# One 512-column matmul for both activation halves in a hybrid decoder trunk, from the first feed-forward on

## The chip, the cores and the metric

One core of a Trainium2 chip runs the whole program. The time is the device time of one execution in microseconds (us), taken as the median of several runs of the same kernel. Lower is better.

## The reference, cut to what matters

Two residual layers over 256 positions of width 2048. Layer 0 mixes with latent attention and gated DeltaNet, layer 1 with gated linear attention (GLA). After each mixer comes a SwiGLU feed-forward of width 5632. Every sub-layer is normalised, then modulated by a shift, a scale and a gate that are linear in SiLU(c).

```python
for layer in range(DEPTH):                      # DEPTH = 2
    shift, scale, gate = ada_modulation(c, ada_w[layer, 0], ada_b[layer, 0])
    h = rms_norm(x, norm_g[layer, 0]) * (1.0 + scale) + shift
    mix = ab_mixer(h, ...) if layer % 2 == 0 else gla_mixer(h, ...)
    x = x + gate * mix
    shift, scale, gate = ada_modulation(c, ada_w[layer, 1], ada_b[layer, 1])
    h = rms_norm(x, norm_g[layer, 1]) * (1.0 + scale) + shift
    x = x + gate * ((silu(h @ w1) * (h @ w3)) @ w2)
return rms_norm(x, final_norm)
```

All of it is float32. D_MODEL is 2048, D_FF is 5632, SEQ is 256.

## The kernel before, in words

**Layout.** Activations are kept transposed: a tile holds 128 features on the partitions and the 256 positions (T = 256) along the free axis. The residual `x` is 16 such tiles.

**Precision.** Every float32 product is made of three matmuls in the float32r format. A weight block w is split into a high part (a cast on ACT, `hi`, L253) and the rest (a subtraction on DVE, `lo`, L193). An activation tile is split likewise and both parts lie side by side in one tile `hl` of shape (128, 2, 256). `mm3` (L261) then issues hi x h0, hi x h1 and lo x h0, each of 256 columns, into the same 256 columns of a PSUM tile. The product lo x h1 is left out.

**Streaming.** `stream_T` (L267) makes 512 output features: it takes four PSUM tiles `acc` of 512 float32 columns each (one bank; the pool has four, so one stream holds them all) and uses the first 256 columns of each. The contraction runs in pieces of four 128-row blocks, called a piece here. For each piece `wload` (L245) starts one DMA of 1 MB (`raw`, three buffers, on SP's queue), casts two halves on ACT and makes two halves of `lo` on DVE (four buffers each for hi and lo, two rows of blocks in one buffer). PE then does, for each of the four output blocks b, four triples `mm3`. So a piece is 48 matmuls. After the last piece of a stream `evac(b, ps)` empties each of the four banks, right after its block. The next stream starts with bank 0.

**The users of `stream_T` from the first feed-forward on.** `ffn` (L1263) runs twice. Its 11 groups of 512 hidden features need one stream over w1 and one over w3, each with 16 blocks of contraction (four pieces). `evac1` applies SiLU from PSUM on ACT; `evac3` multiplies on DVE, then splits the product into h0 (ACT, L223) and h1 (DVE). `ffn2` (L1295) runs w2 in four column groups for 12, 12, 12 and 8 blocks of contraction, and empties with `x_add` (one `scalar_tensor_tensor` on DVE, L200, which adds gate times PSUM to `x`). In layer 1, `gla_in` (L1305) has two streams for q, two for k and four for r (evacuations at L1343, L1345 and L1358); its values come from `gla_v` (L1361), which does not use `stream_T`: there the activation block is the stationary operand, and the weight parts of 512 columns move. `out_proj` (L1243) has four streams with 16 blocks. That makes 2 x (11 x 2 x 64 + 44 x 16) = 4224 triples in the two feed-forwards and 4 x 64 + 4 x 64 + 4 x 64 = 768 in layer 1's mixer, 4992 in all.

**What sets the order.** The rows of `ada_w` (201 MB) are streamed in the background: `tick` is called in every `wload` and steps a generator that issues a DMA of 1 MB (`araw`) on SP's queue and multiplies its rows on DVE (`ada`, L200, two instructions of 1024 columns a step) or on PE. In the first feed-forward its rate is RF0 = 1.5 a piece. Each engine executes in order; the order on each engine is fixed when the kernel is built, by the framework's own estimate of the timeline (`schedule_with_timeline_sim=True`), except that the `ada` steps keep the program's order where `s.keep` is set. At the beginning of each sub-layer `h_tile` makes the 16 `hl` tiles (DVE, ACT for h0, DVE for h1). At the end of layer 0's feed-forward and of both mixers `x_square` squares each new `x` tile on ACT and sums on POOL (`ss`, L193) and PE. The GLA heads (`gla_scores`, `gla_pv`) are woven between the streams of `gla_in`.

Of the kernel before, what the change touches and what calls it, by code (L numbers as in the profile page):

```python
# [13 lines left out]
AF = mybir.ActivationFunctionType  # L14
ALU = mybir.AluOpType
# [4 lines left out]
T = 256  # L20
# [109 lines left out]
class Trunk:  # L130
    def __init__(s, ctx, tc, h, dbg=None, stop=None):
        s.tc, s.nc, s.h, s.dbg, s.stop = tc, tc.nc, h, dbg or {}, stop
        s.cp = ctx.enter_context(tc.tile_pool(name="cp", bufs=1))
        s.rawp = ctx.enter_context(tc.tile_pool(name="rawp", bufs=3))
        s.hlp = ctx.enter_context(tc.tile_pool(name="hlp", bufs=NHL))
        s.arp = ctx.enter_context(tc.tile_pool(name="arp", bufs=NAR))
        s.dp = ctx.enter_context(tc.tile_pool(name="dp", bufs=NDP))
        s.tp = ctx.enter_context(tc.tile_pool(name="tp", bufs=4))
        s.accp = ctx.enter_context(tc.tile_pool(name="accp", bufs=4, space=PSUM))
        s.smp = ctx.enter_context(tc.tile_pool(name="smp", bufs=3, space=PSUM))  # L140
        s.pap = ctx.enter_context(tc.tile_pool(name="pap", bufs=1, space=PSUM))
        s.drp = ctx.enter_context(tc.tile_pool(name="drp", bufs=1, space=bass.MemoryType.DRAM))
        s.n = 0
        s.bg = s.pin = None
        s.mr = None
        s.xg, s.sq = [], []
        s.keep = KP[0]
        s.done = set()
        s.gq = False
        s.fin, s.ends = [], []  # L150
        s.cap = 1 << 30
        s.rate = s.due = 0.0
# [108 lines left out]
    def mm3(s, ps, w, hl, start, stop):  # L261
# [2 lines left out]
        s.mm(ps, w[0], hl[:, 1], False, False)  # L264
        s.mm(ps, w[1], hl[:, 0], False, stop)

    def stream_T(s, src, k0, hs, c0, ncol, evac, nk=None, prepare=None):  # L267

        nb = ncol // 128
        nk = nk or len(hs)  # L270
        ps = [s.acc() for _ in range(nb)]
        for t in range(0, nk, 4):
            n = min(4, nk - t)
            ws = s.wload(src, k0 + t, n, c0, ncol, TI)
            if not TI:
                s.tick(s.rate)
            if prepare is not None:
                prepare(t)
            for b in range(nb):
                for q in range(n):  # L280
                    w = tuple(x[:, b * 128:(b + 1) * 128] for x in ws[q])
                    s.mm3(ps[b][:, :T], w, hs[t + q], t + q == 0, t + q == nk - 1)
                if t + n == nk:
                    evac(b, ps[b][:, :T])
                yield

    def stream_few(s, src, k0, hs, c0, ncol, evac):
# [193 lines left out]


    def x_add(s, l, m, k, ps):
        s.stt(s.x[:, k], ps, s.gate(l, m, k), s.x[:, k], ALU.mult, ALU.add)

    def x_square(s, k):

# [775 lines left out]
    def ffn(s, l):  # L1263
        r = s.x_rstd()
        hs = [s.h_tile(l, 1, k, r) for k in range(KT)]
        s.tick(NF)
        w1, w3, w2 = s.h["ffn_w1"][l], s.h["ffn_w3"][l], s.h["ffn_w2"][l]
        chunks = [(0, 3), (3, 6), (6, 9), (9, 11)]
        pend = None
        for ci, (g0, g1) in enumerate(chunks):  # L1270
            gt = []
            for g in range(g0, g1):
                sl = [None, None]

                def evac1(b, ps):
                    if b % 2 == 0:
                        sl[b // 2] = s.d((128, 2, T))
                    s.act(sl[b // 2][:, b % 2], ps, AF.Silu)
                yield from s.stream_T(w1, 0, hs, 512 * g, 512, evac1)

                def evac3(b, ps):
                    t = sl[b // 2][:, b % 2]
                    s.tt(t, ps, t, ALU.mult)
                    hl = s.d((128, 2, T), F32R)
                    s.split(hl, t)
                    gt.append(hl)
                yield from s.stream_T(w3, 0, hs, 512 * g, 512, evac3)
                if pend is not None:
                    yield from s.ffn2(l, w2, *pend)
                    pend = None  # L1290
            pend = (4 * g0, gt, ci == len(chunks) - 1)
        s.lnexp()
        yield from s.ffn2(l, w2, *pend)
# [11 lines left out]
    def gla_in(s):  # L1305
        nc = s.nc
        w = s.h["gla_w_in"][0]
        r = s.x_rstd()
        s.hs = hs = [s.h_tile(1, 0, k, r) for k in range(KT)]
        s.tick(NF)  # L1310
        def gates():
            ps = s.acc()
            for c in range(4):
                s.stream_narrow([(w, 6144, 16)], 4 * c, hs[4 * c:4 * c + 4], ps, c == 0, c == 3)
            g17 = s.tmp((32, T))
            nc.vector.memset(g17, 1.0)
            nc.vector.tensor_copy(g17[:16], ps[:16, :T])
            wg = [s.d((17, 512)) for _ in range(2)]
            for hf in range(2):
                nc.sync.dma_start(wg[hf][0:16], s.h["gla_w_gk2"][0][:, hf * 512:(hf + 1) * 512])  # L1320
                nc.sync.dma_start(wg[hf][16:17], s.h["gla_b_gk2"][:, hf * 512:(hf + 1) * 512])
            s.ls = {}
            for hf in range(2):
                for t in range(2):
                    p = s.sm()
                    s.mm(p, g17[:17, t * 128:(t + 1) * 128], wg[hf])
                    a = s.d()
                    s.act(a, p, AF.Abs)
                    s.act(a, a, AF.Exp, scale=-1.0)
                    s.act(a, a, AF.Ln, bias=1.0)  # L1330
                    s.stt(a, p, 0.0, a, ALU.min, ALU.subtract)
                    s.ts(a, a, 1.0 / 16.0, ALU.mult)
                    s.ls[hf, t] = a

        s.gq, s.gk, s.gv = {}, {}, {}
        for g in range(2):
            for nme, c0, dst in (("q", 0, s.gq), ("k", 1024, s.gk)):
                def evac(b, ps):
                    key = 2 * g + b // 2
                    if b % 2 == 0:  # L1340
                        dst[key] = s.d((128, 2, T))
                    if nme == "q":
                        s.act(dst[key][:, b % 2], ps, AF.Copy, scale=1.0 / 16.0)  # L1343
                    else:
                        nc.vector.tensor_copy(dst[key][:, b % 2], ps)  # L1345
                yield from s.stream_T(w, 0, hs, c0 + 512 * g, 512, evac)
                if g == 0 and nme == "q":
                    gates()
            yield ("qk", g)
        for g in range(4):  # L1350
            yield from s.gla_v(w, g)
        s.gr = {}
        for g in range(4):
            def evac(b, ps):
                key = 2 * g + b // 2
                if b % 2 == 0:
                    s.gr[key] = s.d((128, 2, T))
                (nc.scalar.copy if b % 2 else nc.vector.tensor_copy)(s.gr[key][:, b % 2], ps)  # L1358
            yield from s.stream_T(w, 0, hs, 4096 + 512 * g, 512, evac)

    def gla_v(s, w, g):  # L1361
# [165 lines left out]
    def run(s):  # L1527
# [43 lines left out]
        if s.stop == "x0":  # L1571
            return
        s.rate = RF0
        s.keep = KP[2]
        s.gq = GQ
        s.cap = 1 << 30
# [66 lines left out]
```

## Time and profile before

| | |
|---|---|
| median of 3 runs | 2623.29 us (2622.99 to 2635.62) |
| the profiled execution's own time | 2625.56 us |
| its span, first to last instruction | 2623.8 us |
| mean granted TensorE clock | 0.988 |
| PE / weight load / DVE / ACT / POOL busy | 98% / 93% / 65% / 44% / 4% |
| moved by DMA | 622.67 MB, mean 237 GB/s |

A busy engine is one with an instruction in flight. Matmuls overlap in the profile: an instruction's duration is longer than the distance from its start to the next one's, so the pace of a stretch is its length divided by its count, not the mean duration. The chain of waits is followed back from the last instruction, so its pieces are the work that set the end.

### The profile page before, as it was taken

What the parts mean: (1) busy time and instruction counts of PE and PEld (TensorE: products, weight loads), DVE (VectorE), ACT (ScalarE), POOL (GpSimd) and SP (SyncE); (2) the same over time, 40 slices, a digit from 0 to 9 for tenths busy, and PEclk for the clock granted to TensorE, in tenths of its full rate; (3) what the DMA queues carried; (4) which work ended last, traced back from release to release, by engine and by line L of the source; (5) the groups of instructions that cost most, each with busy time, mean ns of one, the idle gap of its engine ahead of it and who ended that gap; (6) DMA issues with size and microseconds to landing.
All of it is one profiled execution on the core that took longest, in us unless ns stands there. A gap on an engine that the chain in (4) does not pass through costs nothing.

```text
span 2623.8 us, 48907 instructions
## 1 busy us (share of the span) xinstructions
PE 2571.5 (98%) x20794; PEld 2439.8 (93%) x20794; DVE 1698.8 (65%) x2271; ACT 1157.2 (44%) x1699; POOL 98.9 (4%) x154
## 2 busy tenths in 40 slices
PE   8999998999999999999999999999999999999998
PEld 5799886799999999999998988999999999999998
DVE  3667754688878787777787777865644544544444
ACT  4435664545443343334345434663534334334334
POOL 0000014001000000000011000001000000000001
PEclk9999998999999999999999999999999999999999
DMA  9975666776889888888885555445555555555553
GB/s 348 358 284 165 219 244 254 273 289 222 325 292 344 314 309 317 316 301 316 319 303 209 193 177 192 162 160 177 160 178 187 182 180 190 178 183 188 178 190 115
DMA packets 262280, 622.67 MB, mean 237 GB/s; under 512 B 17119, under 2 KB 28012, under 8 KB 241582
## 3 DMA queue, kind: packets, MB, share of 16 engines
q1 hardware_dynamic: 259902, 608.32, 66.6%
q0 software_dynamic: 1968, 11.14, 1.2%
q8 instruction: 163, 2.67, 0.4%
q14 instruction: 55, 0.45, 0.0%
q10 hardware_dynamic: 192, 0.08, 0.0%
HBM read 616.09 MB, written 3.41 MB: 236 GB/s over the span
## 4 chain that ended last, share of the span: by engine, by line
PE 96%; DVE 2%; ACT 1%; issue 1%; DMA 0%; POOL 0%; SPq 0%; DVEq 0%; ACTq 0%; POOLq 0%
PE acc L190 87%; PE sm L190 6%; PE pa L190 3%; DVE lo L193 1%; ACT hi L253 0%; DVE ada L200 0%; DMA d<-in_x 0%; DMA araw<-in_ada_w 0%; ACT tmp L203 0%; POOL ss L193 0%; PE sm L556 0%; DVE tmp L193 0%; ACT d L203 0%; DVE d L193 0%; POOL d L193 0%
## 5 line engine op out<-in xcount | busy, mean ns | idle before, releaser
L190 PE MATMUL acc<-d,hi 128*128 128x256 f32 x12000 | 2182.6, 285 | 11.0 <-ACT d L203 9.6
L190 PEld LDWEIGHTS acc<-d,hi 128*128 128x128 f32 x12000 | 1871.8, 193 | 46.6 <-ACT d L203 12.8
L190 PE MATMUL acc<-d,lo 128*128 128x256 f32 x6000 | 1685.0, 285 | 3.2 <-DVE lo L193 3.2
L193 DVE TENSOR_TENSOR lo<-raw,hi 128x1024 fp32r<-128x1024 f32 (+2 forms) x801 | 941.6, 1204 | 641.0 <-ACT hi L253 622.1
L253 ACT CAST hi<-raw 128x1024 fp32r<-128x1024 f32 x776 | 782.5, 1046 | 1055.2 <-PE acc L190 912.5
L190 PEld LDWEIGHTS acc<-d,lo 128*128 128x128 f32 x6000 | 1146.4, 193 | 11.9 <-DVE lo L193 4.7
L200 DVE SCALAR_TENSOR_TENSOR ada<-araw,sc,ada 128x1024 f32<-128x1024 f32 x240 | 299.9, 1287 | 6.2 <-DMA araw<-in_ada_w 6.0
L200 DVE SCALAR_TENSOR_TENSOR x<-acc,mod,x 128x256 f32<-128x256 f32 x192 | 87.5, 480 | 66.4 <-PE acc L190 66.4
L193 DVE TENSOR_TENSOR d<-acc,d 128x256 f32<-128x256 f32 (+1 forms) x168 | 79.8, 485 | 64.9 <-PE acc L190 63.1
L190 PE MATMUL acc<-hi,d 128*128 128x512 f32 (+1 forms) x320 | 95.2, 375 | 0.0
L190 PE MATMUL pa<-araw,sc 128*32 128x512 f32 x480 | 73.9, 617 | 3.6 <-DMA araw<-in_ada_w 2.2
L190 PEld LDWEIGHTS acc<-hi,d 128*128 128x128 f32 x320 | 57.8, 189 | 10.7 <-ACT d L1172 0.8
L223 ACT CAST d<-d 128x256 fp32r<-128x256 f32 x128 | 47.8, 404 | 43.6 <-DVE d L193 43.5
L193 DVE TENSOR_TENSOR d<-d,d 128x256 fp32r<-128x256 f32 (+1 forms) x155 | 60.8, 421 | 8.5 <-ACT d L203 4.1
L203 ACT ACTIVATE d<-acc 128x256 f32<-128x256 f32 x96 | 36.7, 382 | 56.6 <-PE acc L190 56.4
L190 PE MATMUL acc<-lo,d 128*128 128x512 f32 (+1 forms) x160 | 59.0, 369 | 0.0
L193 POOL TENSOR_TENSOR ss<-ss,tmp 128x256 f32<-128x256 f32 x44 | 50.5, 1148 | 73.4 <-ACT tmp L203 71.5
L193 DVE TENSOR_TENSOR tmp<-d,tmp 128x512 f32<-128x512 f32 x64 | 43.9, 686 | 6.1 <-issue 3.3
L492 POOL COPY ss<-tmp 128x256 f32<-128x256 f32 x3 | 2.6, 880 | 997.6 <-ACT tmp L203 997.6
L203 ACT ACT_TABLE_LOAD x29 | 37.2, 1283 | 2.2 <-PEq L1632 0.7
L203 ACT ACTIVATE d<-tmp,mod 128x256 fp32r<-128x256 f32 x64 | 29.3, 502 | 20.2 <-DVE tmp L200 15.4
L190 PEld LDWEIGHTS sm<-d,d 32*32 32x32 f32 (+2 forms) x368 | 30.5, 152 | 8.3 <-issue 2.9
(214 smaller groups left out, 1022.9 us busy)
## 6 DMA issues: line engine op xcount, KB each, us to landing
raw<-in_ffn_w SPq DMA_DIRECT2D x264, 1024.0 KB, 5.2
araw<-in_ada_w SPq DMA_DIRECT2D x175, 1024.0 KB, 7.3
raw<-in_gla_w_in SPq DMA_DIRECT2D x48, 1024.0 KB, 5.1
raw<-in_ab_w_in SPq DMA_DIRECT2D x30, 1024.0 KB, 5.3
raw<-in_ab_w_out SPq DMA_DIRECT2D x16, 1024.0 KB, 5.1
raw<-in_gla_w_out SPq DMA_DIRECT2D x16, 1024.0 KB, 5.0
raw<-in_ab_w_in SPq DMA_DIRECT2D x20, 512.0 KB, 7.8
araw<-in_ada_w POOLq DMA_DIRECT2D x9, 1024.0 KB, 5.2
```

The costliest lines, as they stand in the source:

```text
L190: s.nc.tensor.matmul(out, lhsT=lhsT, rhs=rhs, start=start, stop=stop)
L193: (eng or s.nc.vector).tensor_tensor(out=out, in0=a, in1=b, op=op)
L200: return s.nc.vector.scalar_tensor_tensor(out=out, in0=a, scalar=sc, in1=b, op0=op0, op1=op1)
L203: s.nc.scalar.activation(out, a, f, **kw)
L223: s.nc.scalar.copy(hl[:, 0], x)
L253: s.nc.scalar.copy(hi[:, :n, :ncol], raw[:, a:a + n, :ncol])
L492: s.nc.gpsimd.tensor_copy(s.ss, q)
```

## The change

Until the first feed-forward the kernel is as before. From there a flag `s.two` is set. `stream_T` then calls `mmw` for each triple: one matmul of 512 columns, in which the high weight part meets h0 and h1 side by side and fills all 512 columns of the bank, and one of 256 columns, lo x h0, which adds into the first half. For the first contraction block the wide one comes first, for all others the narrow one does. The two halves of the bank are added on emptying: `join` copies the second half on ACT and adds the first on DVE; `x_add` does its instruction once for each half. The evacuations of w1, w3, q, k and r use `join`, with SiLU, the product or the scale applied behind it in SBUF. `gla_v` and everything of layer 0's mixer stay as they are.

```diff
+    def mmw(s, ps, w, hl, first, last):
+        both = hl.rearrange("p a t -> p (a t)")
+        if first:
+            s.mm(ps, w[0], both, True, False)
+            s.mm(ps[:, :T], w[1], hl[:, 0], False, False)
+        else:
+            s.mm(ps[:, :T], w[1], hl[:, 0], False, False)
+            s.mm(ps, w[0], both, False, last)
+
+    def join(s, out, ps):
+        s.nc.scalar.copy(out, ps[:, T:])
+        s.tt(out, ps[:, :T], out, ALU.add)
...
-                    s.mm3(ps[b][:, :T], w, hs[t + q], t + q == 0, t + q == nk - 1)
+                    if two:
+                        s.mmw(ps[b], w, hs[t + q], t + q == 0, t + q == nk - 1)
+                    else:
+                        s.mm3(ps[b][:, :T], w, hs[t + q], t + q == 0, t + q == nk - 1)
                 if t + n == nk:
-                    evac(b, ps[b][:, :T])
+                    evac(b, ps[b] if two else ps[b][:, :T])
...
     def x_add(s, l, m, k, ps):
-        s.stt(s.x[:, k], ps, s.gate(l, m, k), s.x[:, k], ALU.mult, ALU.add)
+        for a in range(0, ps.shape[-1], T):
+            s.stt(s.x[:, k], ps[:, a:a + T], s.gate(l, m, k), s.x[:, k], ALU.mult, ALU.add)
...
-                    s.act(sl[b // 2][:, b % 2], ps, AF.Silu)
+                    a = sl[b // 2][:, b % 2]
+                    if s.two:
+                        s.join(a, ps)
+                        ps = a
+                    s.act(a, ps, AF.Silu)
...
                     t = sl[b // 2][:, b % 2]
+                    if s.two:
+                        u = s.tmp((128, T))
+                        s.join(u, ps)
+                        ps = u
                     s.tt(t, ps, t, ALU.mult)
...
+                    o = dst[key][:, b % 2]
+                    s.join(o, ps)
                     if nme == "q":
-                        s.act(dst[key][:, b % 2], ps, AF.Copy, scale=1.0 / 16.0)
-                    else:
-                        nc.vector.tensor_copy(dst[key][:, b % 2], ps)
+                        s.act(o, o, AF.Copy, scale=1.0 / 16.0)
...
-                (nc.scalar.copy if b % 2 else nc.vector.tensor_copy)(s.gr[key][:, b % 2], ps)
+                s.join(s.gr[key][:, b % 2], ps)
...
         s.rate = RF0
+        s.two = True
```

## Rows read from the trace of the kernel before

**Rows 1.** The page's busy times: us, share of the span, instructions.
```profile
PE 2571.5 (98%) x20794; PEld 2439.8 (93%) x20794; DVE 1698.8 (65%) x2271; ACT 1157.2 (44%) x1699; POOL 98.9 (4%) x154
```

**Rows 2.** The page's chain that ended last, by engine and by line.
```profile
PE 96%; DVE 2%; ACT 1%; issue 1%; DMA 0%; POOL 0%; SPq 0%; DVEq 0%; ACTq 0%; POOLq 0%
```

**Rows 3.** Stages: length, busy us by engine (instructions), PE clock, DMA share, GB/s.
```profile
core 0: us, PE busy (x) PEld busy (x) DVE busy (x) ACT busy (x) POOL busy (x), PEclk, DMA share, GB/s
618.90:1397.00 778.10, 776.02 (x6432) 769.15 (x6432) 610.13 (x646) 311.64 (x390) 16.57 (x12) 1.00 0.85 312
1402.00:1480.00 78.00, 77.42 (x601) 74.61 (x602) 54.66 (x83) 38.73 (x59) 2.27 (x6) 0.96 0.50 170
1480.00:1660.00 180.00, 176.28 (x1094) 159.79 (x1093) 136.01 (x206) 78.16 (x108) 3.55 (x7) 0.98 0.54 183
1660.00:1745.00 85.00, 85.00 (x692) 84.14 (x691) 64.46 (x102) 59.88 (x80) 0.00 (x0) 1.00 0.49 158
1745.00:1845.50 100.50, 96.85 (x798) 95.20 (x797) 58.63 (x79) 48.68 (x74) 13.40 (x12) 1.00 0.55 181
1845.50:2609.00 763.50, 763.45 (x6339) 763.34 (x6339) 377.90 (x442) 310.83 (x395) 10.79 (x12) 1.00 0.55 176
```

**Rows 4.** PE's idle time from 590 us on, by releaser: us, times, longest.
```profile
PE acc L190 <- ACT d L203: 9.4, 3, 3.7
PE sm L190 <- DVE tmp L193: 3.5, 1, 3.5
PE acc L1511 <- ACT d L203: 1.8, 1, 1.8
PE sm L190 <- POOL ss L193: 1.6, 1, 1.6
PE sm L190 <- ACT tmp L436: 1.5, 1, 1.5
PE sm L190 <- ACT tmp L203: 1.4, 2, 1.2
PE acc L190 <- DVE x L200: 0.5, 1, 0.5
```

**Rows 5.** Chain pieces in the feed-forwards (256 columns): start us, us, what.
```profile
918.54 92.25 PE acc L190 x768
...
1845.55 763.40 PE acc L190 x6336
```

**Rows 6.** Chain pieces inside `gla_v` (512 columns, weights moving).
```profile
1583.71 15.45 PE acc L190 x68
...
1600.05 6.36 PE acc L190 x28
```

**Rows 7.** Groups by shape, 1480 to 1660 us: us busy, mean ns | idle before.
```profile
L190 PE MATMUL acc<-hi,d 128*128 128x512 f32 x256 | 82.2, 396 | 0.0
L190 PE MATMUL acc<-lo,d 128*128 128x512 f32 x128 | 50.0, 390 | 0.0
```

**Rows 8.** Groups by shape over the last feed-forward, 1845.5 to 2609 us.
```profile
L200 DVE SCALAR_TENSOR_TENSOR x<-acc,mod,x 128x256 f32<-128x256 f32 x64 | 29.5, 480 | 35.0 <-PE acc L190 35.0
L193 DVE TENSOR_TENSOR d<-acc,d 128x256 f32<-128x256 f32 x44 | 18.0, 423 | 12.4 <-PE acc L190 11.2
L203 ACT ACTIVATE d<-acc 128x256 f32<-128x256 f32 x44 | 16.8, 382 | 25.0 <-PE acc L190 25.0
```

**Rows 9.** DVE's timeline late in layer 0's feed-forward.
```profile
1306.11 2.36 DVE L193 TENSOR_TENSOR lo<-raw,hi 128x1024 fp32r<-128x1024 f32 x2 [0.85 <-ACT hi L253]
1308.39 2.48 DVE L200 SCALAR_TENSOR_TENSOR ada<-araw,sc,ada 128x1024 f32<-128x1024 f32 x2
1311.87 2.36 DVE L193 TENSOR_TENSOR lo<-raw,hi 128x1024 fp32r<-128x1024 f32 x2 [1.00 <-ACT hi L253]
...
1354.52 2.48 DVE L200 SCALAR_TENSOR_TENSOR ada<-araw,sc,ada 128x1024 f32<-128x1024 f32 x2
1356.91 1.66 DVE L200 SCALAR_TENSOR_TENSOR x<-acc,mod,x 128x256 f32<-128x256 f32 x4
1358.48 2.35 DVE L193 TENSOR_TENSOR lo<-raw,hi 128x1024 fp32r<-128x1024 f32 x2
```

**Rows 10.** One stretch of layer 0's feed-forward in which DMA is full (columns as rows 3).
```profile
1310.00:1320.00 10.00, 10.00 (x86) 10.00 (x85) 7.98 (x7) 4.38 (x5) 0.00 (x0) 1.00 1.02 360
```

**Rows 11.** The chain at the end of layer 0's feed-forward.
```profile
1381.22 0.75 DVE x L200 x2
...
1385.73 1.60 POOL ss L193
...
1387.41 1.61 POOL ss L193
...
1389.10 1.59 POOL ss L193
```

**Rows 12.** DVE making h1 in `h_tile`, from 590 us on.
```profile
L200 DVE SCALAR_TENSOR_TENSOR d<-tmp,mod,d 128x256 fp32r<-128x256 f32 x48 | 21.8, 480 | 0.2 <-ACT d L203 0.2
```

**Rows 13.** ACT's timeline in a w1 stream's last piece, layer 0.
```profile
1155.64 0.38 ACT L203 ACTIVATE d<-acc 128x256 f32<-128x256 f32 x1 [1.37 <-PE acc L190]
1156.36 0.38 ACT L203 ACTIVATE d<-acc 128x256 f32<-128x256 f32 x1 [0.34 <-PE acc L190]
1157.56 0.38 ACT L203 ACTIVATE d<-acc 128x256 f32<-128x256 f32 x1 [0.82 <-PE acc L190]
1158.04 2.00 ACT L253 CAST hi<-raw 128x1024 fp32r<-128x1024 f32 x2
1159.94 0.38 ACT L203 ACTIVATE d<-acc 128x256 f32<-128x256 f32 x1
```

More of the change, by code (lines that the diff above doesn't have):

```diff
@@ L148, in __init__ @@
         s.done = set()
-        s.gq = False
+        s.gq = s.two = False
         s.fin, s.ends = [], []
@@ L270, in stream_T @@
         nk = nk or len(hs)
+        two = s.two
         ps = [s.acc() for _ in range(nb)]
```

## The prediction, made before the changed kernel ran

> **What bounds the kernel now.** I read the busy times first. PE has an instruction in flight for 98% of the span, the weight loads for 93%, DVE for 65%, ACT for 44% [rows 1]. Matmuls overlap, so this alone is no proof; the chain of waits is: 96% of the span is PE's own work [rows 2]. By stages, PE is full in both feed-forwards and in most of layer 1's mixer [rows 3], and from 590 us on it idles for some 20 us in all, the longest single wait being 3.7 us [rows 4]. So a shorter sequence on PE shortens the run, as long as what feeds and empties it keeps up. The margins differ by stage: in layer 0's feed-forward DVE is busy for 610 of 778 us (78%) and DMA at 0.85, in the last one DVE for 378 of 764 us (49%) and DMA at 0.55 [rows 3].
>
> **What a matmul costs.** The pace is length over count. With 256 columns it is 92.25 us / 768 = 120.1 ns in layer 0's feed-forward and 763.40 us / 6336 = 120.5 ns over the whole last one, its slow start included [rows 5]. With 512 columns it is 15.45 us / 68 = 227.2 ns, and 6.36 us / 28 = 227.1 ns [rows 6, 7]. Thus 256 more columns cost 107.1 ns, which is 2.4 GHz, and the remainder, 120.1 - 107.1 = 13.0 ns, is paid once for each matmul with its weight load, however wide it is. The columns of a triple stay the same (3 x 256 = 512 + 256); one matmul and one weight load go. The triple before takes 3 x 120.1 = 360.3 ns, after 120.1 + 227.2 = 347.3 ns.
>
> The Trainium skill ("TensorE: Matmul & The Clock Gate", section "Back-to-back issue gap") gives an isolated warm gap of N/2.4 + 2.5 ns, so a fixed part of only 2.5 ns. By it the term below would be 4992 x 2.5 = 12.5 us. The trace disagrees: 120.1 ns at 256 columns, not 109, and the sum goes by the trace.
>
> **The sum, part by part.**
> Triples: 2112 in each feed-forward and 768 in layer 1's mixer, 4992 in all (the 6336 matmuls of the last one are 3 x 2112 [rows 5]). 4992 x 13.0 ns = **-64.9 us**: 27.5 in each feed-forward, 10.0 in the mixer.
>
> Emptying on ACT: one more copy for each block of w1, w3, q, k and some of r, 0.38 us each [rows 8]. In a feed-forward that is 88 x 0.38 = 33 us on an engine that is busy for 312 of 778 us [rows 3]. Its idle time covers that: 0. If the cover were gone, the next stream's first block would wait for its bank (third rival).
>
> Emptying on DVE: in a feed-forward 88 adds of 0.42 us and 64 second `x_add` of 0.48 us [rows 8], 68 us. In the last feed-forward that makes 446 of 735 us, covered. In layer 0's it makes 678 of some 755 us, 90%. Locally it is tighter: one full piece there runs from 1306.11 to 1311.87 us, 5.76 us, of which DVE idles 1.00 [rows 9], so 4.76 us of work. A w2 stream of three such pieces needs 14.3 us, with four `x_add` of 0.41 us (four in 1.66 us [rows 9]) 15.9 of 17.3 us; after the change 14.3 + 3.3 = 17.6 of 16.7 us. It is short by 0.9 us, if `ada` runs in every piece at this density; the mean of 78% says that it doesn't. The split weights are made ahead of PE, so some lateness costs nothing. Bounds: 0, and 0.9 us for each of 16 w2 streams, 14 us. Before, PE waited for an `x_add` there just once, for 0.5 us [rows 4]. Nearer the low end: **+4 us**. What is late then is lo, which `mmw` uses first, and behind it SP's queue: a raw buffer is free only when its lo is done.
>
> DMA: in layer 0's feed-forward 312 GB/s [rows 3] become 312 x 778 / 755 = 322 GB/s. 360 GB/s have been moved in a stretch in which the engines were full and PE never stopped [rows 10]. 0, and the cover is three raw buffers; without it the first rival.
>
> End of layer 0's feed-forward: here the chain leaves PE and runs over `x_add`, the squares and the sum on POOL [rows 11]. A group of four `x_add` grows by 1.6 us, the last block by 0.4, and lo and `ada` stand in the same queue. Bounds: 0 and 16 x 0.41 = 6.6, with the last block 7 to 8 us. I take **+3 us**, about the part that lies on the chain.
>
> Other ends: one `x_add` more behind the last block of the mixer and of the last feed-forward: 2 x 0.41 = **+0.8 us**.
>
> Starts of the three sub-layers: the first matmul now needs h1 too, which DVE makes behind ACT's h0: 0.48 us [rows 12], three times, **+1.4 us**.
>
> Layer 1's mixer: DVE gets 8 adds for q and 8 for r (k's and half of r's replace a copy) and 16 second `x_add`, 14 us on an engine that is at 76% in the woven part (136 of 180 us [rows 3]). Bounds 0 and 6 us; PE waited once for the heads' DVE work there, 3.5 us [rows 4]. **+2 us**.
>
> Order in PE's queue: the first triple of a stream is wide, narrow, all others narrow, wide. No instruction is added and lo came in time before (no wait of PE for lo is left [rows 4]): 0.
>
> Sum: -64.9 + 4 + 3 + 0.8 + 1.4 + 2 = **-53.7 us**. The profiled execution took 2625.6 us (span 2623.8 and 1.8 around it) and would take 2571.9; it lies 2.3 us above the median of 2623.3, so I forecast **2570 us**, -2.0%.
>
> **The rivals.**
> First: layer 0's feed-forward doesn't follow. DVE at 90%, or the transfers behind it, become the bound there, and the 27.5 us of that stage come back. For it: the 0.9 us by which a full w2 stream is short, and the DMA share of 0.85. Against: the stage's mean. -64.9 + 27.5 + 8 (its end) + 0.8 + 1.4 + 4 = -23: 2600 us. Chance 0.11.
>
> Second: PE gains nothing. No row alternates 512 and 256 columns, and none moves an activation tile of 512 columns; if such a matmul costs as much as two narrow ones (or is carried out as two), the triple stays at 360.3 ns and the additions remain: 2623.3 + 11.2 = 2634.5 us, +0.4%. Against: in `gla_v` wide matmuls are single instructions at 227 ns [rows 6, 7]. Chance 0.08.
> By the 2.5 ns of the Trainium skill's page named above it would be 2623.3 - 12.5 + 11.2 = 2622 us, within 0.5% too; [rows 5, 6] speak against it, and its chance is part of this 0.08.
>
> Third, slower: the banks come free too late. `join` needs ACT, then DVE, before a bank is free. ACT executes in order, and at the end of a stream it also has the pair of casts, 2.0 us, which starts only when PE releases the buffers in the stream's last block. Now three SiLUs go ahead of that pair and one behind it [rows 13]. If the order is fixed so that bank 0's copy stands behind the pair, then with the figures of that stretch it starts at 1160.04 and the add ends at 1160.04 + 0.38 + 0.42 = 1160.84 us, while block 3 ends at about 1157.56 + 1.44 = 1159.0 us and PE wants bank 0. That is 1.9 us, and up to 2.4 more if DVE has begun an `ada` pair [rows 9]; at 3.1 us for each of the 52 streams with `join` it is 161 us: 2731 us. It decides from 53.7 / 52 = 1.0 us a stream on; over 1.3 us it is slower by more than 0.5%. Against: in today's order the emptying instructions go as soon as their block is done. Chance 0.06.
>
> **How the numbers follow.** My forecast has 0.75. The range goes down to 2556 us (all of the 64.9 us, the starts paid, and some 4 us of the waits at the end of layer 0's feed-forward, which are retimed, gone too) and up to 2600 us, which is the upper bounds together (-64.9 + 14 + 8 + 0.8 + 1.4 + 6 = -34.7: 2589 us) and the first rival. A change within 0.5% (13 us) is about what can't be told from none. Faster: 0.75 + 0.11 = 0.86; same 0.08; slower 0.06.
>
> **What would show it.** Right: chain pieces in the last feed-forward of some 174 ns for each matmul (347 / 2) and a length of that stage of 734 to 737 us; 12,000 - 2 x 4992 narrow hi matmuls left and 4992 wide ones; DVE near 90% in layer 0's feed-forward, which takes about 755 us up to its end; PE's idle time not above some 30 us. First rival: waits of PE for lo, or of ACT for raw, in that stage, and its length near 775. Second: a triple still at 360 ns. Third: PE waiting for DVE's adds at the beginning of streams, in the last feed-forward too. I am wrong if the last feed-forward, which has room everywhere, does not get shorter by about 27 us.

## The result, and the profile after the change

The changed kernel takes 2686.4 us (median of 4 runs, 2679.2 to 2688.4), the kernel before 2626.0 us (4 runs, 2623.0 to 2635.6): ratio 1.0223, 95% interval 1.0206 to 1.0239. It is **slower** by 2.2%; forecast was 2570 us. The profiled execution spans 2685.6 us.

Three instructions that make `rs` stand at the starts of the three sub-layers, so the stages can be read from VectorE's timeline of the kernel after:

```profile
621.36 0.42 DVE L200 SCALAR_TENSOR_TENSOR rs<-tmp,tmp 128x256 f32<-128x256 f32 x1
...
1474.29 0.42 DVE L200 SCALAR_TENSOR_TENSOR rs<-tmp,tmp 128x256 f32<-128x256 f32 x1
...
1922.41 0.43 DVE L200 SCALAR_TENSOR_TENSOR rs<-tmp,tmp 128x256 f32<-128x256 f32 x1
```

In the profile before they start at 616.39, 1400.97 and 1843.91 us. From one to the next, and from the last to the span's end:

| stage, us | before | after | change | forecast |
|---|---|---|---|---|
| up to the layer-0 feed-forward | 616.4 | 621.4 | +5.0 | 0 |
| layer-0 feed-forward | 784.6 | 852.9 | **+68.3** | -20.0 |
| layer-1 mixer | 442.9 | 448.1 | +5.2 | -7.1 |
| last feed-forward and end | 779.9 | 763.2 | **-16.7** | -26.6 |

The sum is the difference of the spans, 61.8 us. The 5.0 us lie ahead of the change; in the other profiles below the first stage starts anywhere from 617.1 to 621.6 us, so they are scatter. The loss that counts is in the layer-0 feed-forward; the mixer's +5.2, where a gain was forecast, is taken up in e11 and e13. The page after, busy times and the chain by engine:

```profile
PE 2559.8 (95%) x15802; PEld 2185.3 (81%) x15802; DVE 1821.6 (68%) x2607; ACT 1226.7 (46%) x1897; POOL 91.3 (3%) x154
...
PE 86%; DVE 8%; ACT 2%; issue 2%; DMA 1%; POOL 0%; SPq 0%; DVEq 0%; ACTq 0%; POOLq 0%
```

VectorE has 8% of the chain, 2% before [rows 2]. The windows of the three stages (columns as in [rows 3]):

```profile
624.40:1476.60 852.20, 785.40 (x4322) 669.64 (x4322) 667.43 (x808) 345.95 (x483) 10.76 (x13) 0.96 0.78 284
1476.60:1925.10 448.50, 431.14 (x2410) 373.20 (x2410) 326.49 (x499) 231.38 (x342) 17.38 (x24) 0.98 0.52 174
1925.10:2669.60 744.50, 741.95 (x4230) 644.50 (x4230) 432.98 (x588) 340.10 (x477) 11.30 (x12) 1.00 0.53 180
```

PE idles 852.2 - 785.4 = 66.8 us in the first one (2.1 us in the nearest window before [rows 3]), and its mean granted clock is 0.96 instead of 1.00. VectorE is busy for 667 of 852 us, 78%, as before: not full. DMA's share fell from 0.85 to 0.78: transfers are not what is late. The waits name VectorE's `x_add` (us in all, times, longest):

```profile
PE acc L190 <- DVE x L200: 45.5, 14, 7.8
PE acc L190 <- DVE d L193: 7.8, 3, 3.2
...
PE acc L190 <- DVE lo L193: 1.1, 1, 1.1
```

Fourteen times, where the stage has 16 w2 streams; before it was once, 0.5 us [rows 4]. One of them, on VectorE's timeline of the kernel after (a w2 stream ends, PE's last block is done at about 833.3 us):

```profile
824.62 2.36 DVE L193 TENSOR_TENSOR lo<-raw,hi 128x1024 fp32r<-128x1024 f32 x2 [1.09 <-ACT hi L253]
826.90 2.47 DVE L200 SCALAR_TENSOR_TENSOR ada<-araw,sc,ada 128x1024 f32<-128x1024 f32 x2
829.29 2.35 DVE L193 TENSOR_TENSOR lo<-raw,hi 128x1024 fp32r<-128x1024 f32 x2
831.56 2.47 DVE L200 SCALAR_TENSOR_TENSOR ada<-araw,sc,ada 128x1024 f32<-128x1024 f32 x2
833.96 0.47 DVE L200 SCALAR_TENSOR_TENSOR x<-acc,mod,x 128x256 f32<-128x256 f32 x1
834.35 1.21 DVE L193 TENSOR_TENSOR lo<-raw,hi 128x1024 fp32r<-128x1024 f32 x1
835.48 1.26 DVE L200 SCALAR_TENSOR_TENSOR x<-acc,mod,x 128x256 f32<-128x256 f32 x3
836.66 1.21 DVE L193 TENSOR_TENSOR lo<-raw,hi 128x1024 fp32r<-128x1024 f32 x1
837.79 1.65 DVE L200 SCALAR_TENSOR_TENSOR x<-acc,mod,x 128x256 f32<-128x256 f32 x4
```

Here the planner (the framework's own estimate of the timeline, which fixes the order on each engine) put the first halves of all four banks first (one, then three), then the four second halves. So bank 0, the one that PE wants next, is free only after the **fifth** `x_add`, at about 838.2 us, with two lo between. In nine of the 14 waits PE goes on right behind the fifth `x_add` of the stream. Before, each `x_add` frees its bank, bank 0's with the first, whether the four stand in one run [rows 9], as in 11 of the 16 streams, or with lo and `ada` between. PE's timeline there:

```profile
838.41 0.76 PE L190 MATMUL acc<-d,hi 128*128 128x512 f32 x1 [5.06 <-DVE x L200]
...
840.04 0.63 PE L190 MATMUL acc<-d,hi 128*128 128x512 f32 x1
...
840.68 0.63 PE L190 MATMUL acc<-d,hi 128*128 128x512 f32 x1
...
848.66 0.28 PE L190 MATMUL acc<-d,lo 128*128 128x256 f32 x1
...
849.01 0.28 PE L190 MATMUL acc<-d,lo 128*128 128x256 f32 x1
...
863.17 0.76 PE L190 MATMUL acc<-d,hi 128*128 128x512 f32 x1 [5.51 <-DVE x L200]
```

After standing still for 5.06 us, PE makes a triple in 0.64 us (840.04 to 840.68), by 848.66 in 0.35 us. The windows show the granted clock beside it (the third number from the right):

```profile
836.00:841.00 5.00, 2.59 (x8) 2.33 (x9) 3.44 (x7) 0.00 (x0) 0.00 (x0) 0.52 0.92 345
841.00:846.00 5.00, 5.00 (x25) 4.25 (x25) 0.00 (x0) 0.00 (x0) 0.00 (x0) 0.80 0.32 121
846.00:858.00 12.00, 11.65 (x67) 9.85 (x65) 9.82 (x10) 5.36 (x6) 0.00 (x0) 1.00 0.43 151
```

1.00 is the level of 2.4 GHz; 0.52 is almost all at the level of 1.2 GHz (768 columns in 0.64 us). So a late bank can cost twice: a stream of 48 triples takes 863.17 - 838.41 = 24.8 us, of which PE stands still for 5.5 us and loses some 2 us by running at the lower level (24.8 - 5.5 - 48 x 0.3535 = 2.3). The trace has the clock at that level in 12 stretches of this stage, with PE busy in them for 46.6 us (before: 3.4 us). Eight of the 12 begin in one of the 14 waits or at most 1.5 us behind it; after the other six the clock stayed up.

The pace of the new triple (chain pieces: start, us, what; the fourth is a w2 stream of the last feed-forward):

```profile
949.33 62.35 PE acc L190 x352
...
1185.97 92.56 PE acc L190 x524
...
1925.18 196.70 PE acc L190 x1120
...
2121.99 16.99 PE acc L190 x96
...
2173.37 150.66 PE acc L190 x864
```

In the last feed-forward 150.66 / 432 = 348.8 ns (forecast 347.3, before 361.4 by 763.40 / 2112 [rows 5]). In the layer-0 feed-forward, in stretches without a wait, 62.35 / 176 = 354.3 and 92.56 / 262 = 353.3 ns, so only 7 ns are gained there.

### The profile page after: what moved, and what is told of

Its sections match the earlier page's. It is cut to its first block, busy times and chain, and to the rows that moved or that the text cites. A ratio compares the mean times of both kernels' runs of the same rounds, so it can differ in the third digit from the quotient of the medians.

```text
span 2685.6 us, 39255 instructions
## 1 busy us (share of the span) xinstructions
PE 2559.8 (95%) x15802; PEld 2185.3 (81%) x15802; DVE 1821.6 (68%) x2607; ACT 1226.7 (46%) x1897; POOL 91.3 (3%) x154
## 4 chain that ended last, share of the span: by engine, by line
PE 86%; DVE 8%; ACT 2%; issue 2%; DMA 1%; POOL 0%; SPq 0%; DVEq 0%; ACTq 0%; POOLq 0%
PE acc L190 79%; PE sm L190 5%; DVE lo L193 3%; DVE ada L200 2%; PE pa L190 2%; ACT hi L253 1%; DVE x L200 1%; DMA araw<-in_ada_w 0%; DVE tmp L193 0%; DVE d L200 0%; DVE tmp L200 0%; DVE d L193 0%; ACT tmp L203 0%; DMA d<-in_x 0%; DMA d<-in_ada_w 0%
## 5 line engine op out<-in xcount | busy, mean ns | idle before, releaser
L190 PE MATMUL acc<-d,hi 128*128 128x512 f32 (+2 forms) x7008 | 2137.9, 369 | 71.4 <-DVE x L200 46.2
L190 PE MATMUL acc<-d,lo 128*128 128x256 f32 x6000 | 1635.6, 284 | 4.3 <-DVE lo L193 4.3
L190 PEld LDWEIGHTS acc<-d,hi 128*128 128x128 f32 (+1 forms) x7008 | 1244.1, 191 | 309.6 <-issue 73.3
L200 DVE SCALAR_TENSOR_TENSOR x<-acc,mod,x 128x256 f32<-128x256 f32 x336 | 147.4, 477 | 38.7 <-PE acc L190 37.6
L193 DVE TENSOR_TENSOR d<-acc,d 128x256 f32<-128x256 f32 (+1 forms) x200 | 92.7, 474 | 71.5 <-PE acc L190 40.3
L203 ACT ACTIVATE d<-d 128x256 f32<-128x256 f32 (+1 forms) x138 | 63.0, 467 | 46.6 <-DVE d L193 26.0
L280 ACT COPY d<-acc 128x256 f32<-128x256 f32 x120 | 43.8, 370 | 45.1 <-PE acc L190 43.1
L280 ACT COPY tmp<-acc 128x256 f32<-128x256 f32 x88 | 32.5, 370 | 33.5 <-PE acc L190 33.4
L203 ACT ACTIVATE tmp<-x 128x256 f32<-128x256 f32 x64 | 26.0, 413 | 42.7 <-DVE x L200 42.1
L203 ACT ACTIVATE tmp<-tmp 128x512 f32<-128x512 f32 (+2 forms) x47 | 26.9, 573 | 33.6 <-DVE tmp L193 25.7
```

What stands on the lines that cost most here:

```text
L190: s.nc.tensor.matmul(out, lhsT=lhsT, rhs=rhs, start=start, stop=stop)
L193: (eng or s.nc.vector).tensor_tensor(out=out, in0=a, in1=b, op=op)
L200: return s.nc.vector.scalar_tensor_tensor(out=out, in0=a, scalar=sc, in1=b, op0=op0, op1=op1)
L203: s.nc.scalar.activation(out, a, f, **kw)
L280: s.nc.scalar.copy(out, ps[:, T:])
```

## The experiments

Two theories stood at the outset. A: the banks of the w2 streams come free late, because of where their readers stand in VectorE's list. B: VectorE, which also does the `ada` work, has too much to do in the layer-0 feed-forward.

All times in us; stages as in the table above, from one profiled execution each, so that their sum is not the median; each ratio is against runs of the kernel before on the same chip, with its 95% interval.

| run | layer-0 ff | mixer | last ff | median | ratio |
|---|---|---|---|---|---|
| before | 784.6 | 442.9 | 779.9 | 2626.0 | 1 |
| after | 852.9 | 448.1 | 763.2 | 2686.4 | 1.0223 [1.0206, 1.0239] |
| e1 last ff only | 785.7 | 444.9 | 762.6 | 2613.3 | 0.9952 [0.9934, 0.9971] |
| e2 pairs by bank | 858.1 | 454.4 | 761.6 | 2694.3 | 1.0259 [1.0240, 1.0279] |
| e3 w2 narrow | 793.9 | 453.1 | 766.2 | 2630.4 | 1.0009 [0.9994, 1.0024] |
| e4 x_add from a copy | 798.8 | 454.9 | 767.3 | 2640.3 | 1.0058 [1.0039, 1.0076] |
| e5 first streams narrow | 850.8 | 448.1 | 763.7 | 2682.2 | 1.0206 [1.0191, 1.0221] |
| e6 all banks by ScalarE | 789.8 | 455.2 | 773.2 | 2638.8 | 1.0040 [1.0026, 1.0055] |
| e7 ada rate 1.0 | 789.5 | 462.1 | 782.5 | 2652.6 | 1.0094 [1.0077, 1.0111] |
| e8 = e5 + e6 + e7 | 780.0 | 476.2 | 781.1 | 2659.8 | 1.0120 [1.0105, 1.0136] |
| e9 best mix | 781.4 | 443.7 | 766.9 | 2610.0 | **0.9923 [0.9902, 0.9944]** |
| e10 one reader | 802.8 | 452.2 | 759.2 | 2635.9 | 1.0029 [1.0015, 1.0044] |
| e11 mixer only | 787.7 | 451.6 | 779.6 | 2636.9 | 1.0032 [1.0020, 1.0045] |
| e12 no second x_add | 785.8 | 453.6 | 763.5 | 2619.6 | 0.9959 [0.9944, 0.9974] |
| e13 out_proj only | 784.7 | 441.7 | 779.0 | 2625.6 | 0.9996 [0.9982, 1.0010] |
| e14 e1, last w2 narrow | 785.6 | 448.0 | 761.7 | 2610.7 | 0.9951 [0.9933, 0.9969] |

How far a stage's length scatters is seen where its code is that of before: the layer-0 feed-forward 784.6 to 787.7 (five profiles), the mixer 442.9 to 448.0 (four), the last feed-forward 779.0 to 779.9 (three).

**e1: wide in the last feed-forward alone.**
```diff
-        s.two = True          # after s.rate = RF0
+        s.two = True          # before drain(s.ffn(1))
```
(q, k and r are emptied as before where `s.two` is false.)

> The wide matmul is used in layer 1's feed-forward alone, where DVE has room. Both theories: that stage takes about 744 us as in the changed kernel, against 763.5 before, and nothing else moves: about 2626 - 19 = 2607 us. If the wide matmul were no cheaper on PE, the time would stay at 2626 or rise.

2613.3 us, with a last stage of 762.6, as in the changed kernel: the gain there is independent of the rest, and smaller than the 27.5 us that were forecast. This alone is faster than both kernels.

**e2: x_add in pairs, bank by bank.**
```diff
+            ins = s.stt(...)
+            if s.two and a == 0 and k % 4:
+                s.tc.keep_in_program_order(ins)
```

> Changed kernel, with the same instructions; only DVE's order is bound so that a bank's two x_add stand before the next bank's first one (in the changed kernel all four first halves come first, so that bank 0 is freed after five x_add and the lo instructions between them). Theory A (order: bank 0 is freed late): layer 0's feed-forward gets 15 to 40 us shorter, 2646 to 2671 us in all; not all of it, since lo instructions still stand between bank 0's two. Theory B (load: DVE has too much work in that stage in any order): within 10 us of the changed kernel, 2676 to 2696.

2694.3 us: no gain, which by what was expected is theory B's range. The order did change as meant: in ten of the 11 waits for `x_add` that are left in the stage, PE goes on right behind the stream's second one, no longer the fifth. But lo and `ada` still stand between the two `x_add` of bank 0 (at the place shown above two lo, and the wait there falls only from 5.06 to 3.89 us), and the waits add up to 39.3 us instead of 45.5. So the bank comes nearly as late as in the changed kernel, and this run alone can't tell A from B. e10 puts the question again.

**e3: three matmuls in all w2 streams of both feed-forwards.**
```diff
+            s.two = False
             yield from s.stream_T(w2, k0, gt, 512 * cg, 512, evac)
+            s.two = True
```

> Changed kernel, but the w2 streams use three narrow matmuls and one x_add again. The PE gain of 2 x 704 = 1408 triples is given up (1408 x 12 ns = 17 us). Theory A: the waits for the second x_add go, w1, w3 and GLA keep their gain: 2590 to 2605 us. Theory B: the joins alone (37 us more DVE work in layer 0's feed-forward) still hold PE up: 2615 to 2650.

2630.4 us: 56 of the 60 us come back. But the layer-0 feed-forward, with wide w1 and w3, is still 9 us longer than before.

**e4: x_add from a whole copy that ScalarE makes of the bank.**
```diff
+        u = s.tmp()
+        s.nc.scalar.copy(u, ps)
-            s.stt(s.x[:, k], ps[:, a:a + T], ...)
+            s.stt(s.x[:, k], u[:, a:a + T], ...)
```

> Changed kernel, but for x_add ACT copies the whole bank of 512 columns to SBUF and DVE's two x_add read from there, so that ACT alone frees the bank; DVE has as much work as in the changed kernel. Theory A: PE no longer waits for x_add: 2570 to 2600 us. Theory B: DVE is as loaded as before, PE then waits for lo: over 2650.

2640.3 us, between the two. VectorE has as many `x_add` as in the changed kernel, but reads no bank there, and the stage gets 54 us shorter. So its load alone is not the cause; that the bank waits for it is. From about 1354 us on, the end of the stage, the chain leaves PE and runs largely over lo and `ada`, ScalarE's copies, the `x_add` and ScalarE's squares.

**e5: the first stream of each stage narrow.**
```diff
+                s.two = g > 0
                 yield from s.stream_T(w1, 0, hs, 512 * g, 512, evac1)
+                s.two = True          # and so for the first q stream
```

> Only the first weight stream of each of the three stages (the first w1 stream of both feed-forwards, the first q stream of the mixer) goes back to three matmuls of 256 columns. Theory S (a 512-column first matmul needs the second activation part at once, and VectorE makes those one by one while TensorE waits and loses its clock): each stage start gets 3 to 6 us shorter, 2666 to 2677 us, and the waits of TensorE for the activation tiles at 622, 1476 and 1925 us fall from 2 to 5 us each to under 2. Rival (the start is set by VectorE's list of activation tiles, whichever part is used first): no change, 2680 to 2690 us.

2682.2 us, the rival's range. From `rs` to the first matmul the three starts take 2.5, 1.6 and 1.6 us again, 0.5 to 1.1 us less than in the changed kernel; in the lengths of the stages this can't be told from scatter.

**e6: every wide bank copied whole by ScalarE, joins included.**
```diff
     def join(s, out, ps):
-        s.nc.scalar.copy(out, ps[:, T:])
-        s.tt(out, ps[:, :T], out, ALU.add)
+        u = s.tmp()
+        s.nc.scalar.copy(u, ps)
+        s.tt(out, u[:, :T], u[:, T:], ALU.add)
```

> Each wide bank is copied whole by ScalarE to a tile (x_add and the other emptyings), VectorE then works from that tile alone; the number of VectorE instructions is unchanged. Theory A (what costs the time is that banks are freed by VectorE, whose queue is in order and late): better than the kernel in which only x_add was changed so, 2640 us: 2610 to 2632 us, and TensorE's waits for VectorE's join in the layer-0 feed-forward and the mixer are gone. Rival B (VectorE has too much work in these stages, wherever the bank is freed): 2636 to 2646 us, with TensorE's waits now on the weights' low parts.

2638.8 us, rival B's range. Against e4, the joins' part gains 9 us in the layer-0 feed-forward (798.8 to 789.8), where PE no longer waits for a join, but for lo 5.2 us instead of 4.1; and the last feed-forward loses 6 (767.3 to 773.2), 10 against the changed kernel. Why that one gets longer stays open.

**e7: ada work spread otherwise.** `RF0, RG = 1.0, 1.0` instead of `1.5, 0.5`.

> The changed kernel with the interleaved ada work spread otherwise: 1.0 instead of 1.5 steps per weight load in the layer-0 feed-forward and 1.0 instead of 0.5 in the mixer. Theory B (VectorE's load in the layer-0 feed-forward is what makes the banks late): some 60 of 186 ada steps of 1.2 us leave that stage, its w2 streams recover, 2640 to 2670 us. Theory A (only the order in which a bank's two additions stand in VectorE's list counts): 2680 to 2692 us.

2652.6 us, theory B's range. 124 instead of 186 `ada` instructions of 1.28 us stand in the layer-0 feed-forward, and it falls by 63 us. The mixer takes 60 instead of 24 of them and gets 14 us longer; the last stage takes 26 instead of none and gets 19 longer.

**e8: e5, e6 and e7 together.**

> The three edits of the other kernels of this set together: ScalarE frees every wide bank, the first streams are narrow, the ada work is spread evenly. If bank release, stage starts and VectorE's load are the three causes and add up: 2580 to 2605 us, faster than the kernel before, with the layer-0 feed-forward at 755 to 770 us and the mixer at 435 to 443. If one of them is not a cause, or a fourth is there: above 2612 us.

2659.8 us, a clear miss: the layer-0 feed-forward comes to 780.0, but the mixer to 476.2. PE waits there 12.7 us for ScalarE's products of the heads, 7.3 at a time. The edits don't add up; that each takes from an engine that the next one needs is the likely reason, not a measured one.

**e9: best mix.**
```diff
+        if s.l0:                      # layer-0 feed-forward: as e6
+            ...
+        else:
+            s.nc.vector.tensor_reduce(out=out, in_=ps.rearrange("p (a t) -> p t a", a=2), ...)
+                s.two = l == 1 or g > 0        # w1
+            s.two = l == 1                     # w2
```
(`x_add` as in e10, `s.two` off in the mixer.)

> Meant as the best mix: wide in the last feed-forward (a bank is emptied by one VectorE reduction that adds the halves, so that no ScalarE copy is added) and in w1 and w3 of the layer-0 feed-forward except its first stream (banks freed by a whole ScalarE copy); w2 of the layer-0 feed-forward and the whole mixer stay at three matmuls. If the layer-0 feed-forward can keep the gain of its w1 and w3 streams once VectorE frees no bank late: that stage 766 to 774 us instead of 784.6, the mixer 443 to 446, the last one 757 to 762 instead of 779.9, together 2588 to 2602 us. If the joins alone fill VectorE in that stage: 785 to 795 us for it and 2608 to 2622 us.

2610.0 us, 0.9923 of the kernel before and faster than both kernels, but short of what was expected in both feed-forwards. In the first one PE idles for 6.7 us in all, as little as before (6.9), and still only 3 us are gained. Two rows account for them: the slower pace of the wide triple there, 1344 x 7.0 ns = 9.4 us instead of 17.5, and `ada`'s own matmuls, which take 13.2 us instead of 6.4 (last section).

**e10: two VectorE instructions as before, but only one reads the bank.**
```diff
+        u = s.tmp((128, T))
+        s.nc.vector.tensor_reduce(out=u, in_=ps.rearrange("p (a t) -> p t a", a=2), ...)
+        s.stt(s.x[:, k], u, s.gate(l, m, k), s.x[:, k], ALU.mult, ALU.add)
```

> The changed kernel; x_add adds the two halves with one VectorE reduction into a tile and then adds the gated tile to x: two VectorE instructions for each bank as in the changed kernel, but only the first one reads the bank, so a bank is free after one instruction, as in the kernel before. Theory A (the second reader of the bank, far down VectorE's list, is what frees it late): the layer-0 feed-forward falls from 852.9 to 785 to 800 us, 2615 to 2640 us in all. Theory B (VectorE's load, however the bank is read): 835 to 860 us for that stage, 2670 to 2695 us.

2635.9 us. This decides between A and B. VectorE's timeline at the place shown above, in this kernel:

```profile
830.09 2.47 DVE L200 SCALAR_TENSOR_TENSOR ada<-araw,sc,ada 128x1024 f32<-128x1024 f32 x2
832.48 0.68 DVE L509 TENSOR_REDUCE tmp<-acc 128x256 f32<-128x512 f32 x1
833.08 1.21 DVE L193 TENSOR_TENSOR lo<-raw,hi 128x1024 fp32r<-128x1024 f32 x1
834.21 1.88 DVE L509 TENSOR_REDUCE tmp<-acc 128x256 f32<-128x512 f32 x3
836.01 1.21 DVE L193 TENSOR_TENSOR lo<-raw,hi 128x1024 fp32r<-128x1024 f32 x1
837.14 1.67 DVE L200 SCALAR_TENSOR_TENSOR x<-tmp,mod,x 128x256 f32<-128x256 f32 x4
```

The reductions stand where the four first `x_add` stood, the `x_add` where the four second ones did (this timeline runs 1.5 us ahead of the other); bank 0 is free at 833.1 us instead of 838.2. And the waits of PE in that stage:

```profile
PE acc L190 <- DVE tmp L509: 10.6, 10, 1.8
```

10.6 us instead of 45.5, though VectorE does more work (684.8 us busy instead of 667.4, since a reduction takes 683 ns and the `x_add` behind it 538, where each of the two `x_add` took 476). So 852.9 - 802.8 = 50 us are the price of the second reader; the stage came 3 us above the range that theory A gave. That e7 gains as much is no evidence for load as such: with fewer `ada` instructions the list ahead of the second readers is shorter, so they too come earlier (PE's waits for `x_add` there: 18.2 us).

**e11: wide in the mixer alone**, `s.two` set before the mixer and cleared after it.

> Wide matmuls in the layer-1 mixer alone (q, k, r and the output projection), both feed-forwards as before. The prediction's terms for the mixer were 10 us gained and 2 us for its emptying: 2612 to 2620 us. If the joins put ScalarE and VectorE behind in the woven heads, as the changed kernel's mixer of 448.1 us against 442.9 says: 2627 to 2636 us.

2636.9 us, 10 more (5 to 12 by the interval) instead of 8 less; the mixer takes 451.6. The waits of PE in it, beside those of before in [rows 4], where 3.5 us is all for the heads on VectorE and 1.4 on ScalarE:

```profile
PE sm L190 <- DVE tmp L193: 6.0, 2, 4.2
PE sm L190 <- ACT tmp L203: 5.4, 3, 4.7
```

**e12: no second x_add in the layer-0 feed-forward** (so the product of the high weight part with the low activation part isn't added there).
```diff
+        n = T if (l, m) == (0, 1) else ps.shape[-1]
+        for a in range(0, n, T):
```

> The changed kernel without the second x_add in the layer-0 feed-forward: there the high weight part times the low activation part isn't added in the w2 streams, so x is a little off; the matmuls are all still issued. VectorE has one instruction for each bank again. If the second x_add (as a reader of the bank and as load together) is the whole loss of the w2 streams: the layer-0 feed-forward at 775 to 790 us instead of 852.9, 2610 to 2625 us. If the 512-column matmuls or the joins of w1 and w3 are at fault as well: over 800 us, 2635 us or more.

2619.6 us, as expected: 67 us of the stage hang on these 64 instructions, 50 of them, by e10, on where they release the bank; the other 17 were not divided further. The joins and 512-column matmuls alone leave the stage where it was (785.8).

**e13: wide in the output projection alone.** `s.two` set just before `out_proj` of the mixer.

> Wide matmuls in the mixer's output projection alone (256 of the mixer's 768 triples); q, k, r and both feed-forwards as before. Theory W (the mixer loses in its woven part, where q, k and r are joined beside the heads): the output projection keeps its gain of about 3 us less some tenths at its streams' ends, the mixer takes 439 to 442 us against 442.9 to 444.9, 2622 to 2627 us in all. Rival (the loss sits in the output projection, whose x_add reads each bank twice): the mixer takes 447 to 452 us, 2631 to 2637 us.

2625.6 us with a mixer of 441.7: theory W. The output projection loses nothing (a gain of 3 us would not stand out from the scatter of 442.9 to 448.0), so the loss is in the woven part with q, k and r. That the heads' small matmuls stand in PE's queue behind products that ScalarE and VectorE now make later is read from the waits of e11; no run tests it.

**e14: e1 with the four last w2 streams narrow.** `s.two = l == 1 and not last` in `ffn2`.

> Wide in the last feed-forward alone, as in the first of these experiments (its last stage took 762.6 us against 779.9), but with the four last w2 streams at three matmuls and one x_add each. They give up 128 triples of 12.7 ns, 1.6 us. Theory E (the 6.4 and 2.8 us that TensorE stands still in these streams come from the second x_add of each bank and its output work behind it): the stage 755 to 760 us, 2605 to 2610 us. Rival (they come from the joins just before, which put ScalarE's table load and the casts of the first w2 piece late): 761 to 765 us, 2611 to 2617 us.

2610.7 us, a stage of 761.7, no different from e1's 762.6. The expectation rested on a misreading: the chain of e1 leaves PE for 6.4 and 2.8 us in those streams, but the windows over them show PE busy all the same, in e1 (first row) and in e14 (second):

```profile
2556.00:2598.00 42.00, 40.84 (x233) 34.91 (x232) 26.43 (x41) 22.41 (x39) 11.26 (x12) 1.00 0.28 100
...
2508.00:2601.00 93.00, 92.88 (x653) 86.72 (x652) 51.63 (x69) 47.63 (x77) 10.94 (x12) 1.00 0.46 153
```

In e1 1.2 us idle, and no more, was there to win. A piece of the chain on another engine is a way that the dependences run, and not yet idle time of PE.

## Why the prediction was wrong

**The step that failed** is "Emptying on DVE ... +4 us", bounds 0 and 14. It priced the second `x_add` as load: a w2 stream "short by 0.9 us". What it costs is 67 us in that stage (e12), 50 of it not load at all (e10). The question that was not put is which instruction frees the bank, and what stands before it on VectorE. Before, a bank had one reader; after, two, and the planner put the four first readers ahead of the four second ones, with lo between. [Rows 4] (0.5 us) say how little bank release cost with one reader, and were read as a bound for two.

**The third rival** named this mechanism (banks free too late, a chain of instructions in a fixed queue) and a price of 3.1 us each, but at the wrong place: at `join`, with ScalarE's copy behind its casts. The joins cost PE 7.8 + 2.3 us in the layer-0 feed-forward; the w2 streams, which that rival left out, 45.5 us in 14 waits, and the lower clock at eight of them. Its chance of 0.06 and the sum's 4 us had the same root.

**The first rival's place** was right, its reason not: the stage gives back far more than its 27.5 us, while neither lo (1.1 us of waits) nor DMA (share 0.78) is late. Its mark, a "length near 775", was passed by 78 us. (Its sum takes 4 us that it doesn't name; with the mixer's 2 in their place it gives 2598, not 2600.)

**Triples, -64.9 us.** In the last feed-forward 12.7 of 13.0 ns are there (361.4 to 348.8). In the layer-0 feed-forward only 7 ns (353.3 to 354.3): 14.8 of 27.5 us. So even with every bank free in time, that stage could not have reached 755 us; e8 and e9 stop at 780 and 781. The second rival's warning ("no row alternates 512 and 256 columns") was half right. By the Trainium skill's rule that the prediction weighed ("TensorE: Matmul & The Clock Gate", section "Back-to-back issue gap") the last feed-forward would, by an estimate from its 2.5 ns, have gained 2112 x 2.5 ns = 5.3 us; it gained 19.0 from its first to its last `acc` matmul, so the trace speaks against the rule here too.

**"I am wrong if the last feed-forward does not get shorter by about 27 us"**: its matmuls end 744.4 us after the first instead of 763.4, 19.0 us less. 2112 x 12.7 ns are 26.8. The missing 8 us: the first pieces (196.70 - 560 x 0.3488 = 1.4), the ends of 12 w2 streams (16.99 + 0.10 - 48 x 0.3488 = 0.35 each, 4.2 in all: the second `x_add` again, though VectorE is at 58%; in e10, with one reader, this stage takes 759.2 us, 4.0 less), and the last four streams (41.4 us for 112 triples, 2.3 over).

**Mixer, -10 + 2.** Over nine profiles with the wide mixer and the old `ada` rates it takes 448.1 to 455.2 us, mean 452.4; over four with the narrow one 442.9 to 448.0, mean 444.9. So +7.5 instead of -8. The load argument (136 of 180 us) failed here too. The waits of e11 suggest the same reason, that an engine with room may still deliver late what PE's queue has next; where the 7.5 us go was not shown.

**Right:** ScalarE's copies at 0 in the last feed-forward (no wait of PE for a joined bank there), DMA at 0, the order of the triples (1.1 us of waits for lo), the starts (from `rs` to the first matmul 2.5, 1.6 and 1.6 us became 3.0, 2.4 and 2.8, in all +2.4 against 1.4; e5 agrees), the last end (+1.1 from the last `acc` matmul to the span's end, against 0.4).

**End of layer 0's feed-forward, +3 us**, bounds 0 and 8: mis-sized. From the first matmul of its four last w2 streams to the next `rs` it takes 67.8 us instead of 55.0, so +12.8; PE waits there for 10.4 us instead of 2.7, 3.0 of them for `ada` and 5.5 for `x_add`.

The balance of the stage: -14.8 (pace) + 59.9 (idle 66.8 instead of 6.9 us between the stage's first matmul and the next one's, 783.7 us of which PE was busy for 776.8 before) + 23.2. The last number is the remainder of 68.3, and the lower clock makes most of it. PE is busy at that level for 46.6 us; at 0.64 us a triple instead of 0.354 that loses an estimated 46.6 x (1 - 0.354 / 0.64) = 20.8 us, against 1.5 of its 3.4 us before. `ada`'s own matmuls take 8.4 us instead of 6.4.

## What to carry to other kernels

When a change makes a buffer be read twice, ask which instruction now frees it, and what the planner will put before that one; how busy the engine is on average does not tell (78% before and after here). Let the first reader take everything out of the bank (one reduction, or a copy), and let the second work from SBUF: the same number of instructions, 50 us less here. A gain per instruction measured in one stage is checked in each stage where it is claimed, since its pace may differ there.

## What the runs showed of the hardware

A wide triple has two paces. In PE's timeline of the kernel after, lo matmuls follow each other after 0.353 us at 848.66 us (shown above: 849.01 - 848.66, and 24 triples in 8.48 us to 857.14), and after 0.347 us in a w2 stream of the last feed-forward:

```profile
2137.42 0.28 PE L190 MATMUL acc<-d,lo 128*128 128x256 f32 x1
...
2138.46 0.27 PE L190 MATMUL acc<-d,lo 128*128 128x256 f32 x1
```

(three triples in 1.04 us.) Both at a granted clock of 1.00. Behind its first piece most streams keep one of two patterns to their end: lo matmuls that start 0.345 and 0.348 us apart in turn, or 0.345, 0.356 and 0.359. The second stands in most streams of the layer-0 feed-forward of the kernel after, the first in most of its last one, and the same stage has another mix in another kernel: 348.8 ns in the last feed-forward of the kernel after, 353.8 in that of e9 (a piece of 723.08 us with 4088 matmuls). Narrow triples had one pace, 360 to 361 ns, in every stage. What sets it stays open; no run was made for it.

Small matmuls that stand together run together. `ada` ends in groups of eight matmuls of 128*32. In the kernel before (first row, the chain) eight in a row take 0.99 us: four start within 0.02 us, the other four 0.43 us behind them. In e9 (second row, PE's timeline) the planner put other work between some of them, and two alone, which start 0.45 us apart, take 1.04 us. So the 48 of the layer-0 feed-forward cost 13.2 us instead of 6.4.

```profile
764.71 0.99 PE sm L190 x8
```
```profile
987.61 1.04 PE L190 MATMUL sm<-ada,cst 128*32 128x512 f32 x2
```

The Trainium skill ("TensorEngine Tiling (Array Packing)", section "Available Configurations") gives four independent tiles for 128x32; the trace of the first row, with four starting together, agrees. The second row shows that two left alone take as long as eight that are neighbours in PE's queue.
